# More products by seven in the MLP's down projection, sums of weights made sooner, activations by pairs of chunks

## Chip, cores, metric

The kernel runs on one core of one Trainium2 chip. The metric is device microseconds (us) of one execution, the median of several runs. Its engines go by their short names in the profile: PE is TensorE's matmul and PEld its weight load, DVE is VectorE, ACT is ScalarE, POOL is GpSimd, SP is SyncE, which issues nearly all DMAs.

## What is computed

One encoder block over 256 tokens of 2048 features, in float32, of which the reference's body is this:

```python
h = rms_norm(x, attn_norm[i])
proj = h @ w_in[i]
qa, ka, va, qb, kb, vb, ga, gb = jnp.split(proj, split_points, axis=-1)
ya = windowed_gqa(qa, ka, va, rel_bias_table, sink_a[i])
yb = dilated_attention(qb, kb, vb, rel_bias_table)
merged = jax.nn.sigmoid(ga) * (ya @ w_branch_a[i]) + jax.nn.sigmoid(gb) * (yb @ w_branch_b[i])
x = x + merged @ w_out[i]
hf = rms_norm(x, ffn_norm[i])
g = dwconv_centred(hf @ w_ffn_gate[i], conv_w[i], conv_b[i])
x = x + (jax.nn.gelu(g) * (hf @ w_ffn_up[i])) @ w_ffn_down[i]
gate_p = jax.nn.sigmoid(rms_norm(x, ple_norm[i]) @ w_ple_gate[i])
x = x + gate_p * (p[i] @ w_ple_proj[i])
return rms_norm(x, final_norm)
```

The change touches the last six lines: the gated MLP (2048 to 5632 and back, with a convolution of width 3 over the tokens on the gate's path and a tanh form of gelu), the embedding p (256 features) with its gate, and the last norm.

## The kernel before

**Number format.** Every operand of a matmul is split into a high part that TensorE multiplies in one pass and a low part, the remainder: ScalarE copies the high part out of a float32 tile (`nc.scalar.activation(hi, src, AF.Copy)`, line 264), VectorE subtracts it (line 265). A product takes three matmuls (`thirds`, lines 365 to 367: high by high, high by low, low by high), or two in the E stages (line 308 512 columns wide, line 315 256 wide).

**Stages.** The weights come as a list of pieces of 128 x 2048 values (1 MB), grouped by stages that TensorE does in order: A (input projections and attention), B0 to B3 with ba and bb (branch gates and projections), D0 and D1 (w_out), then twice, for each half of the 44 chunks of the MLP, E (gate and up products, `mlp` behind each) and F0, F1 (down projection to the left and the right half of the 2048 columns): E0, F00, F01, E1, F10, F11. At the end stand pp0 and pp1 (p by w_ple_proj) and G0, G2, G3 (the gate of p).

**Products by seven.** B, D, F and G0 are stages of quads: a piece is a 2 x 2 block of weights for two chunks of features and two strips of 512 columns. A piece marked s is multiplied directly: eight products, 24 matmuls of 512 columns. A piece marked S uses Strassen's scheme in Winograd's form: seven products, 21 matmuls. It pays with sums. Of the weights, VectorE makes four units out of a raw tile instead of two: unit n of 512 columns, unit n of 1024, then three differences in place (lines 257 to 259, one 1024 wide, two 512 wide), and units T13 and T24 of 1024 each. Of the activations, `sums_of` makes four sums of a pair of chunks. Of the results, `row_sums` adds the accumulators M1, M5, M6, M7 at the stage's end. An s piece needs the accumulators M2, M3, M4 and P22 alone, an S piece M1 to M7. `DOWN = "SsSsSsSsSss"` gives the eleven pairs of each F stage their kinds.

**Buffers that order the work.** PSUM has eight banks, each a tag with one buffer: M2 0, M3 1, M4 2, M1 3, M7 4, M5 5, M6 6, P22 7. A new tile in a bank waits until the last reader of the tile before it is done. Units of weights have rings: six of kind n (names uh, ul), two of kind T (vh, vl); raw tiles have three buffers. `pump` makes the next unit whenever a slot is dropped. Pieces of work that belong to another stage are hung up with `at((stage, piece, product), f)` and issued there by `run_due`; a scheduler then arranges each engine's instructions, whose queues run in order.

**Around the end.** xr holds the rows (2 x 128 tokens x 2048). When F10 has finished the left half of xr, `rows_pair` turns it back into columns: per group of two chunks four transposes on TensorE into one bank, then for each chunk ScalarE writes the high part of pl (line 472) and VectorE the low part (line 473). The four groups of the left half are hung up in F11 at (0,6), (1,2), (1,5) and (2,1) and all use the bank of P22; the four of the right half come at pp0, through M2, M3, M4 and P22. `combine` makes the sums of pl's pairs for G0, in a tile named pair with two buffers. `load_last` loads p (256 KB) into a tile of the name pair at piece 2 of F10, and `split_last` splits it at piece 9 into small tiles t and u. `quads("F11", ...)` has its own accumulator P22, opened by its first s piece, and reads it in line 936 (`residual`'s `finish`) behind the last matmul.

**The tail.** G3's last two products for the second 128 tokens are done in two halves of 256 columns, so that the left half is ready before the right. Behind them come, per 128 tokens, tanh, the addition into xr, squares, the sum `known`, the gains (line 1115), v (line 1112), the power on POOL (line 1114), the scaling by r and the output.

Of the kernel before, what the change touches and what calls it, by code (L numbers as in the profile page):

```python
# [16 lines left out]
P = 128  # L17
T = 256
# [70 lines left out]
JOINT = 4  # L89
JOINED = 2  # L90
# [4 lines left out]
DOWN = "SsSsSsSsSss"  # L95
# [3 lines left out]
def _ffn(half):  # L99

    jobs = []
    for f in range(FHALF + 1):
        if f < FHALF:
            jobs.append(("g", half * FHALF + f))
        if f:
            jobs.append(("u", half * FHALF + f - 1))
    return jobs


def _pieces():  # L110
# [29 lines left out]
    for half in range(2):  # L140
# [6 lines left out]
        for s in range(2):  # L147
            quads("F%d%d" % (half, s), ("w_ffn_down", 2 * s * WIDE), ("w_ffn_down", (2 * s + 1) * WIDE),
                  DOWN, half * FHALF)
# [38 lines left out]
def _encoder(ctx: ExitStack, tc, xt, pt, xrow, cols, gainrow, table, onehot, mask, ident_in, wts, out):  # L188
# [58 lines left out]
    def produce():  # L247
# [7 lines left out]
        if kind == "T13":  # L255
            q = [raw[:, i * WIDE:(i + 1) * WIDE] for i in range(4)]
            nc.vector.tensor_tensor(raw[:, :2 * WIDE], raw[:, WIDE:3 * WIDE], raw[:, :2 * WIDE], op=ALU.subtract)  # L257
            nc.vector.tensor_tensor(q[2], q[2], q[0], op=ALU.subtract)
            nc.vector.tensor_tensor(q[3], q[3], q[2], op=ALU.subtract)
# [6 lines left out]
        made[u] = (hi, lo)  # L266
        state["unit"] = u + 1
# [94 lines left out]
    def thirds(acc, stationary, w, first, last):  # L362

        (sh, sl), (wh, wl) = stationary, w
        nc.tensor.matmul(acc, sh, wh, start=first, stop=False, skip_group_check=True)  # L365
        nc.tensor.matmul(acc, sh, wl, start=False, stop=False, skip_group_check=True)  # L366
        nc.tensor.matmul(acc, sl, wh, start=False, stop=last, skip_group_check=True)  # L367
# [4 lines left out]
    def quad_stage(stage, moving, combos=None, tags=("M2", "M3", "M4", "P22")):  # L372
# [24 lines left out]
        for i, p in enumerate(pieces):  # L397
# [24 lines left out]
    def wide_stage(stage, moving, names, joint=1):  # L422
# [3 lines left out]
        ends = []  # L426
        alone = len(pieces) - joint
        for i, span in [(i, 1) for i in range(alone)] + [(alone, joint)]:
            g = 0
            for t in range(2):  # L430
                for c in range(4 * span):
# [5 lines left out]
                    if 1 < joint == span and t and c >= 4 * span - 2:  # L437
                        ends.append((part(moving(k), t), w))
                        continue
# [3 lines left out]
            for h in range(2) if ends else ():  # L443
                for e, (stationary, w) in enumerate(ends):
                    cs = slice(h * T, (h + 1) * T)
                    thirds(accs[1][:, cs], stationary, [a[:, cs] for a in w], False, e == 1)
            if ends:
                drop(_UNITS_OF[pieces[-1]][1])
# [4 lines left out]
    def gather(acc, scale=1.0, u=None, keep=lambda ins: ins):  # L453
# [3 lines left out]
        if u is None:  # L457
            u = sc.tile([P, T], F32, name="u")
# [32 lines left out]
    def diagonal(r):  # L491

        dg = sc.tile([P, T], F32, name="rdg", bufs=1)
# [75 lines left out]
    for step in order:  # L569
# [9 lines left out]
        while 4 * done + 5 < state["at"] // FIRST:  # L579
# [278 lines left out]
    def combine(key, m, pair, tag):  # L858

        u = held["tok"].tile([P, 2, T], F32, name="pair", bufs=2)  # L860
# [112 lines left out]

    def mlp(kind, n, acc):
        tok = held["tok"]
        if kind == "g":
            if n % 2 == 0:
                held["gw"] = tok.tile([P, 4, T], F32, name="gw", tag="c%d" % (n // 2 % 2 + 1))
            c, w = (held["gw"][:, 2 * (n % 2) + i] for i in range(2))
            u = gather(acc)  # L980
            nc.vector.tensor_tensor(u, u, rt[1], op=ALU.mult)
            nc.vector.tensor_scalar(c, u, tap(1, n), tap(3, n), op0=ALU.mult, op1=ALU.add)
            nc.vector.scalar_tensor_tensor(c[:, 1:], u[:, :-1], tap(0, n), c[:, 1:], op0=ALU.mult, op1=ALU.add)
            nc.vector.scalar_tensor_tensor(c[:, :-1], u[:, 1:], tap(2, n), c[:, :-1], op0=ALU.mult, op1=ALU.add)
            nc.scalar.activation(w, c, AF.Square)
            nc.vector.tensor_scalar(w, w, 0.044715, 1.0, op0=ALU.mult, op1=ALU.add)
# [191 lines left out]
```

## Time and profile before

| | |
|---|---|
| median of 3 runs | 1457.38 us (1457.35 to 1457.71) |
| profiled execution | 1457.96 us, of which 1456.2 us is the span from the first to the last instruction |
| granted TensorE clock, mean | 0.998 |
| busy PE, DVE, ACT | 1444.5, 1248.8, 822.1 us |
| E0, F00 with F01, E1 | about 628 to 875, 875 to 988, 988 to 1233 us |
| F10 with F11 | about 1233 to 1347 us |
| last matmul | at 1445.64 us |

In a row of the timeline stand the start in us, the duration in us, the engine, the line, the operation, the output and the inputs by name, the shape and how many instructions the row joins; in square brackets the idle time before it and what ended it. Engines with a q behind their name (SPq, ACTq) are issuing DMAs. Durations of neighbouring instructions on an engine overlap by some tens of ns, so what an instruction costs its engine is read from start to start. A row of windows gives for a stretch its length and each engine's busy time with the number of instructions in brackets.

### The profile page before, as it was taken

The numbers are of one execution on the slowest core, as the hardware profiler recorded it, in microseconds if no ns is written. First come the engines' busy times: TensorE is split into PE (matmuls) and PEld (weight loads), VectorE is DVE, ScalarE is ACT, GpSimd is POOL, SyncE is SP. The second block draws the span as 40 slices with busy tenths as digits, with TensorE's granted clock in tenths as the row PEclk, the third lists the DMA queues.
The fourth block names the chain that finished last, engine by engine and source line by source line (L and its number), as shares of the span: only waits on it lengthen the run. The fifth ranks groups of instructions, "written<-read, shape, count | busy, mean of one in ns | idle before, by whom it ended". The sixth has DMA issues, their size and how long they took to land.

```text
span 1456.2 us, 19520 instructions
## 1 busy us (share of the span) xinstructions
PE 1444.5 (99%) x7488; PEld 1235.9 (85%) x7488; DVE 1248.8 (86%) x1849; ACT 822.1 (56%) x1141; POOL 4.1 (0%) x9
## 2 busy tenths in 40 slices
PE   9999999999999999999999999999999999999997
PEld 8888888888888888888888888888888888888785
DVE  7677665679998989989888899989888889999995
ACT  7455544446555656666555555455555555565762
POOL 0000000000000000000000000000000000000000
PEclk9999999999999999999999999999999999999999
DMA  9654444535546456465554545565555554546462
GB/s 335 249 206 146 152 168 175 175 141 203 192 187 235 180 213 234 174 232 193 186 199 175 202 152 221 176 254 183 199 184 193 185 192 173 193 191 234 170 237 81
DMA packets 46312, 282.88 MB, mean 194 GB/s; under 512 B 4932, under 2 KB 9668, under 8 KB 13964
## 3 DMA queue, kind: packets, MB, share of 16 engines
q1 hardware_dynamic: 45500, 280.46, 53.2%
q8 instruction: 58, 0.95, 0.3%
q10 hardware_dynamic: 720, 1.19, 0.2%
q14 instruction: 34, 0.28, 0.1%
HBM read 279.49 MB, written 2.14 MB: 193 GB/s over the span
## 4 chain that ended last, share of the span: by engine, by line
PE 97%; DVE 1%; ACT 1%; issue 1%; DMA 0%; SPq 0%; POOL 0%; POOLq 0%; DVEq 0%; ACTq 0%
PE bank L308 29%; PE bank L315 15%; PE bank L365 14%; PE bank L366 14%; PE bank L367 14%; PE bank L354 2%; PE bank L356 2%; PE bank L355 2%; PE bank L292 1%; PE bank L293 1%; PE bank L870 1%; PE bank L687 0%; PE bank L635 0%; PE bank L634 0%; PE bank L633 0%
## 5 line engine op out<-in xcount | busy, mean ns | idle before, releaser
L264 ACT ACTIVATE uh<-raw 128x1024 fp32r<-128x1024 f32 (+2 forms) x518 | 522.3, 1017 | 399.5 <-PE bank L308 183.6
L265 DVE TENSOR_TENSOR ul<-raw,uh 128x1024 fp32r<-128x1024 f32 (+2 forms) x518 | 596.8, 1169 | 128.9 <-ACT uh L264 68.8
L308 PE MATMUL bank<-hf,uh 128*128 128x512 f32 x1408 | 336.3, 391 | 0.0
L308 PEld LDWEIGHTS bank<-hf,uh 128*128 128x128 f32 x1408 | 258.9, 188 | 50.2
L315 PEld LDWEIGHTS bank<-hf,ul 128*128 128x128 f32 x1408 | 180.4, 191 | 6.7
L315 PE MATMUL bank<-hf,ul 128*128 128x256 f32 x1408 | 182.8, 283 | 0.0
L264 ACT ACTIVATE vh<-raw 128x1024 fp32r<-128x1024 f32 x92 | 97.4, 1058 | 57.0 <-DVE raw L257 25.4
L265 DVE TENSOR_TENSOR vl<-raw,vh 128x1024 fp32r<-128x1024 f32 x92 | 111.9, 1219 | 0.4
L308 PE MATMUL bank<-hs,uh 128*128 128x512 f32 x432 | 103.6, 392 | 0.0
L456 ACT ACTIVATE t<-bank 128x256 f32<-128x256 f32 x122 | 46.5, 384 | 96.6 <-PE bank L315 89.5
L308 PEld LDWEIGHTS bank<-hs,uh 128*128 128x128 f32 x432 | 79.5, 188 | 15.6
L365 PE MATMUL bank<-uh,act 128*128 128x512 f32 x232 | 90.4, 390 | 0.0
L366 PE MATMUL bank<-ul,act 128*128 128x512 f32 x232 | 90.4, 390 | 0.0
L367 PE MATMUL bank<-uh,act 128*128 128x512 f32 x232 | 90.3, 389 | 0.0
L365 PE MATMUL bank<-uh,hs 128*128 128x512 f32 x172 | 67.3, 391 | 0.0
L367 PE MATMUL bank<-uh,hs 128*128 128x512 f32 x172 | 67.3, 391 | 0.0
L366 PE MATMUL bank<-ul,hs 128*128 128x512 f32 x172 | 67.1, 390 | 0.0
L257 DVE TENSOR_TENSOR raw<-raw 128x1024 f32<-128x1024 f32 x46 | 56.1, 1221 | 0.6
L315 PE MATMUL bank<-hs,ul 128*128 128x256 f32 x432 | 56.6, 284 | 0.0
L315 PEld LDWEIGHTS bank<-hs,ul 128*128 128x128 f32 x432 | 54.5, 191 | 1.0
L366 PE MATMUL bank<-vl,S 128*128 128x512 f32 x138 | 54.1, 392 | 0.1
L365 PE MATMUL bank<-vh,S 128*128 128x512 f32 x138 | 54.1, 398 | 0.0
(240 smaller groups left out, 2273.2 us busy)
## 6 DMA issues: line engine op xcount, KB each, us to landing
raw<-in_wts SPq DMA_DIRECT2D x251, 1024.0 KB, 4.8
raw<-in_wts SPq DMA_DIRECT2D x12, 512.0 KB, 7.2
xr<-in_xrow SPq DMA_DIRECT2D x4, 512.0 KB, 8.3
x<-in_xt SPq DMA_DIRECT2D x13, 128.0 KB, 6.0
hb<-hold SPq DMA_DIRECT2D x3, 514.0 KB, 5.9
hb<-hold SPq DMA_DIRECT2D x2, 768.0 KB, 7.5
last<-in_gainrow SPq DMA_DIRECT2D x1, 1024.0 KB, 6.9
out<-xr SPq DMA_DIRECT2D x4, 256.0 KB, 2.6
```

The source lines that it names most:

```text
L257: nc.vector.tensor_tensor(raw[:, :2 * WIDE], raw[:, WIDE:3 * WIDE], raw[:, :2 * WIDE], op=ALU.subtract)
L264: nc.scalar.activation(hi, src, AF.Copy)
L265: nc.vector.tensor_tensor(lo, src, hi.bitcast(F32), op=ALU.subtract)
L308: nc.tensor.matmul(acc, weights(u)[0][:, o * P:(o + 1) * P], m, start=first, stop=False, skip_group_check=True)
L315: nc.tensor.matmul(acc[:, T:], weights(u)[1][:, o * P:(o + 1) * P], m[:, :T], start=False, stop=last, skip_group_check=True)
L354: nc.tensor.matmul(acc[:, :n * P], xh, hi, start=(k == 0), stop=False)
L355: nc.tensor.matmul(acc[:, :n * P], xh, lo, start=False, stop=False)
L356: nc.tensor.matmul(acc[:, :n * P], xl, hi, start=False, stop=(k == KC - 1))
L365: nc.tensor.matmul(acc, sh, wh, start=first, stop=False, skip_group_check=True)
L366: nc.tensor.matmul(acc, sh, wl, start=False, stop=False, skip_group_check=True)
L367: nc.tensor.matmul(acc, sl, wh, start=False, stop=last, skip_group_check=True)
L456: keep(nc.scalar.activation(t, acc[:, T:], AF.Copy, scale=scale))
```

## The change

1. `DOWN` becomes a table by half and strip: F00, F01 and F10 get SSsSsSsSsSs (six S of eleven, the first two in a row), F11 gets sSsSsSsSsSs (five S, s first). The sums of activations are made for the pairs 0, 1, 3, 5, 7, 9. In all, nine matmuls of 512 fewer.
2. The differences of weights of an S piece are issued when its second unit n is made, no longer when the first unit T is.
3. M4 comes ahead of M2 and M3 in an S piece.
4. `mlp` works on pairs of chunks: products are gathered one by one, but the convolution, gelu and the split are done for two chunks at once; the first tap goes from VectorE to ScalarE. An up product comes two gate products later instead of one (LAG).
5. The tile pair has one buffer instead of two. p is loaded at piece 5 of F11 and split at piece 10, into one tile p in the place of S4.
6. G3's half columns go. In the tail, v is computed ahead of the gains, in program order.
7. Small: u of `gather` and the tile rdg have other buffers; squares in the first norm come later.

```diff
-DOWN = "SsSsSsSsSss"
+DOWN = (("SSsSsSsSsSs", "SSsSsSsSsSs"), ("SSsSsSsSsSs", "sSsSsSsSsSs"))
+PAIRS = (0, 1, 3, 5, 7, 9)
...
-        if kind == "T13":
-            q = [raw[:, i * WIDE:(i + 1) * WIDE] for i in range(4)]
-            nc.vector.tensor_tensor(raw[:, :2 * WIDE], raw[:, WIDE:3 * WIDE], raw[:, :2 * WIDE], op=ALU.subtract)
...
         made[u] = (hi, lo)
+        if _PIECES[p][0] == "S" and u == _UNITS_OF[p][1]:
+            q = [raw[:, i * WIDE:(i + 1) * WIDE] for i in range(4)]
+            nc.vector.tensor_tensor(raw[:, :2 * WIDE], raw[:, WIDE:3 * WIDE], raw[:, :2 * WIDE], op=ALU.subtract)
...
-                        ("M6", sums[1], 3, 0, None), ("M2", part(b, 0), 1, 1, None), ("M3", sums[3], 1, 0, 1),
-                        ("M4", part(b, 1), 3, 1, 3))):
+                        ("M6", sums[1], 3, 0, None), ("M4", part(b, 1), 3, 1, 3),
+                        ("M2", part(b, 0), 1, 1, None), ("M3", sums[3], 1, 0, 1))):
...
-        u = held["tok"].tile([P, 2, T], F32, name="pair", bufs=2)
+        u = held["tok"].tile([P, 2, T], F32, name="pair", bufs=1)
...
     def load_last():
-        held["pr"] = held["tok"].tile([P, 2, T], F32, name="pair", bufs=2)
+        held["pr"] = held["tok"].tile([P, 2, T], F32, name="pair", bufs=1)
         keep(nc.sync.dma_start(held["pr"], pt))
 
     def split_last():
-        for k in range(2):
-            ph_.append(sc.tile([P, T], FR, name="t"))
-            pl_.append(sc.tile([P, T], FR, name="u"))
-            nc.scalar.activation(ph_[k], held["pr"][:, k], AF.Copy)
-            nc.vector.tensor_tensor(pl_[k], held["pr"][:, k], ph_[k].bitcast(F32), op=ALU.subtract)
+        h = held["tok"].tile([P, 2, 2, T], FR, name="p", tag="S4")
+        held["p"] = h
+        nc.scalar.activation(h[:, 0], held["pr"], AF.Copy)
+        nc.vector.tensor_tensor(h[:, 1], held["pr"], h[:, 0].bitcast(F32), op=ALU.subtract)
...
-            at(("F10", 2, 0), load_last)
-            at(("F10", 9, 0), split_last)
+            at(("F11", 5, 0), load_last)
+            at(("F11", 10, 0), split_last)
...
-        nc.vector.tensor_scalar(v, ssq[:, t, 4:], known[:, t:t + 1], 1.0 / D, op0=ALU.add, op1=ALU.mult)
+        keep(nc.vector.tensor_scalar(v, ssq[:, t, 4:], known[:, t:t + 1], 1.0 / D, op0=ALU.add, op1=ALU.mult))
         r = sc.tile([P, 1], F32, name="r3")
         nc.gpsimd.tensor_tensor(r, v, mhalf[:, :1], op=ALU.pow)
-        nc.vector.tensor_tensor(xr[:, t, cut[3]], xr[:, t, cut[3]], gains[:, cut[3]], op=ALU.mult)
+        keep(nc.vector.tensor_tensor(xr[:, t, cut[3]], xr[:, t, cut[3]], gains[:, cut[3]], op=ALU.mult))
```

What it moves, engine by engine. First TensorE at the end of F11, before: bank_11899 is P22, bank_12299 and bank_12307 are pp0's, bank_11919 is the fourth group's.

```order
L367 MATMUL bank_11899<-uh_12169,act2_8950 128x512
L365 MATMUL bank_12299<-uh_12178,t_11713 128x512
L366 MATMUL bank_12299<-ul_12179,t_11713 128x512
L367 MATMUL bank_12299<-uh_12178,u_11714 128x512
L365 MATMUL bank_12299<-uh_12197,t_11717 128x512
L366 MATMUL bank_12299<-ul_12198,t_11717 128x512
L367 MATMUL bank_12299<-uh_12197,u_11718 128x512
L365 MATMUL bank_12307<-uh_12178,t_11713 128x512
L366 MATMUL bank_12307<-ul_12179,t_11713 128x512
L367 MATMUL bank_12307<-uh_12178,u_11714 128x512
L870 MATMUL bank_11919<-ident_75,xr_4916 128x128 x4
```

pp0 follows F11 at once; one group of the left half stands nine matmuls into it. The same place after the change: bank_11587 is P22, bank_11615, bank_11649 and bank_11671 are the second, third and fourth group of the left half, bank_12071, bank_12085 and bank_12097 are groups of the right half, bank_12233 and bank_12237 are G0's.

```order
L369 MATMUL bank_11587<-uh_11923,act2_8835 128x512
L862 MATMUL bank_12071<-ident_75,xr_4919 128x128
L862 MATMUL bank_12085<-ident_75,xr_4919 128x128
L862 MATMUL bank_12097<-ident_75,xr_4919 128x128
L862 MATMUL bank_11615<-ident_75,xr_4919 128x128 x4
L862 MATMUL bank_11649<-ident_75,xr_4919 128x128 x4
L862 MATMUL bank_12071<-ident_75,xr_4919 128x128 x3
L862 MATMUL bank_12085<-ident_75,xr_4919 128x128 x3
L862 MATMUL bank_12097<-ident_75,xr_4919 128x128 x3
L862 MATMUL bank_11671<-ident_75,xr_4919 128x128 x4
L367 MATMUL bank_12233<-uh_12037,pl_11556 128x512
L368 MATMUL bank_12233<-ul_12038,pl_11556 128x512
```

After fifteen matmuls of G0, with the last group (bank_12111) among them, pp0 begins with `L367 MATMUL bank_12056<-uh_11953,p_11992 128x512`. Three groups of the left half have moved behind F11, and pp0 behind them.

Second, VectorE behind F11 after the change, from the reading of P22 (line 928) on. pair_11775 is the tile of pl's pair 2, c_11996 a sum of accumulators.

```order
L928 TENSOR_TENSOR xr_4919<-xr_4919,bank_11587 128x512
L267 TENSOR_TENSOR raw_11951<-raw_11951 128x512
L262 TENSOR_TENSOR vl_12045<-raw_11951,vh_12044 128x1024
L465 SCALAR_TENSOR_TENSOR pl_11556<-bank_11615,cl_73,pl_11556 128x256
L268 TENSOR_TENSOR raw_11951<-raw_11951 128x512
L465 SCALAR_TENSOR_TENSOR pl_11556<-bank_11615,cl_73,pl_11556 128x256
L930 TENSOR_TENSOR xr_4919<-xr_4919,c_11996 128x1024
L262 TENSOR_TENSOR vl_12049<-raw_11951,vh_12048 128x1024
L465 SCALAR_TENSOR_TENSOR pl_11556<-bank_11649,cl_73,pl_11556 128x256
```

Before the change the rows of pl for the second and third group stood in F11; here they are spread over VectorE's other work behind it.

Third, SyncE around p's load after the change:

```order
L246 DMA raw_11964<-in_wts 128x2048
L246 DMA raw_12031<-in_wts 128x2048
L246 DMA raw_12123<-in_wts 128x2048
L1015 DMA pair_11810<-in_pt 128x512
L246 DMA raw_12183<-in_wts 128x2048
L1055 DMA last_12055<-in_gainrow 128x2048
```

and before it:

```order
L244 DMA raw_11396<-in_wts 128x2048
L244 DMA raw_11431<-in_wts 128x2048
L1006 DMA pair_11441<-in_pt 128x512
L244 DMA raw_11475<-in_wts 128x2048
L244 DMA raw_11509<-in_wts 128x2048
```

The load has moved down the queue from F10 to just ahead of the gains' load, with one raw tile between them; its tile pair_11810 takes the buffer of pair_11775.

More of the change, by code (lines that the diff above doesn't have):

```diff
@@ L101, in _ffn @@
     jobs = []
-    for f in range(FHALF + 1):
+    for f in range(FHALF + LAG):
         if f < FHALF:
             jobs.append(("g", half * FHALF + f))
-        if f:
-            jobs.append(("u", half * FHALF + f - 1))
+        if f >= LAG:
+            jobs.append(("u", half * FHALF + f - LAG))
     return jobs
```

97 lines of the change are left out of this document (52 added, 45 removed).

## The prediction

> **What bounds the kernel now.** I read the page first: the busy line and the chain that ended last.
>
> ```profile
> PE 1444.5 (99%) x7488; PEld 1235.9 (85%) x7488; DVE 1248.8 (86%) x1849; ACT 822.1 (56%) x1141; POOL 4.1 (0%) x9
> PE 97%; DVE 1%; ACT 1%; issue 1%; DMA 0%; SPq 0%; POOL 0%; POOLq 0%; DVEq 0%; ACTq 0%
> ```
>
> TensorE carries 97% of the chain. The view of the waits, asked for TensorE alone, leaves nothing else:
>
> ```profile
> PE bank L225 <- DVE mhalf L220: 1.1, 1, 1.1
> PE bank L293 <- DVE ul L265: 0.3, 1, 0.3
> ```
>
> So between its start and the last matmul TensorE waits 1.4 us in all, and the end moves only by matmuls taken away, by waits newly made, and by the tail behind the last matmul. The windows by stage say how close VectorE follows (columns: length, then busy time and count of PE, PEld, DVE, ACT, POOL; granted clock, DMA share, GB/s). The four stretches are E0, F00 with F01, E1, F10 with F11:
>
> ```profile
> 628.00:875.00 247.00, 247.00 (x1427) 218.33 (x1427) 219.42 (x394) 142.03 (x216) 0.71 (x1) 1.00 0.53 189
> 875.00:988.00 113.00, 113.00 (x500) 93.43 (x500) 103.12 (x115) 60.76 (x67) 0.00 (x0) 1.00 0.57 210
> 988.00:1233.00 245.00, 245.00 (x1410) 216.56 (x1409) 216.70 (x379) 136.11 (x203) 0.00 (x0) 1.00 0.53 187
> 1233.00:1346.00 113.00, 113.00 (x505) 93.34 (x504) 107.92 (x132) 66.52 (x80) 0.00 (x0) 1.00 0.56 206
> ```
>
> TensorE is full in all four; VectorE has 28 us to spare in each E stage, 10 in F00 with F01, 5 in F10 with F11. A matmul of 512 columns takes 113.00 / 500 = 0.226 us.
>
> **The change part by part.**
>
> *MLP activations by pairs, LAG.* They take VectorE work out of E0 and E1, where 247.00 and 245.00 us of TensorE stand over 219.42 and 216.70 of VectorE. No matmul goes, so the worth is nothing. The cover is those 28 us; were it gone, the cost would show as TensorE waits in E, and the work only shrinks there.
>
> *Three more products by seven.* F00, F01 and F10 each turn one s piece (24 matmuls) into an S (21): 9 x 0.226 = -2.0 us on TensorE. VectorE pays for it. Its pace is read from start to start in the rows behind F11, which the largest term needs as well:
>
> ```profile
> 1347.38 0.68 DVE L936 TENSOR_TENSOR xr<-xr,bank 128x512 f32<-128x512 f32 x1
> 1347.97 0.68 DVE L265 TENSOR_TENSOR ul<-raw,uh 128x512 fp32r<-128x512 f32 x1
> 1348.58 0.68 DVE L936 TENSOR_TENSOR xr<-xr,bank 128x512 f32<-128x512 f32 x1
> 1349.18 1.22 DVE L257 TENSOR_TENSOR raw<-raw 128x1024 f32<-128x1024 f32 x1
> 1350.31 1.21 DVE L265 TENSOR_TENSOR ul<-raw,uh 128x1024 fp32r<-128x1024 f32 x1
> 1351.44 0.47 DVE L473 SCALAR_TENSOR_TENSOR pl<-bank,cl,pl 128x256 fp32r<-128x256 f32 x1
> 1351.84 0.68 DVE L258 TENSOR_TENSOR raw<-raw 128x512 f32<-128x512 f32 x1
> ```
>
> A 1024-wide operation costs 1.13 us of VectorE, a 512-wide one 0.61, a row of pl 0.40. An S piece has four of the first kind and three of the second, 6.35; an s piece has two of the first, 2.26; each exchange adds 4.1. In F00 with F01 VectorE then has 103.12 + 8.2 = 111.3 us against 113.00 - 1.4 = 111.6 of TensorE: no slack. The stages now begin with two S in a row, behind the other stage's finishing adds. At F00's start the rings are full, since VectorE was early in E0; at F01's they are not. I take +1.0 us for the boundaries, from 0 (the rings hold enough) to 3. The sums made sooner, and M4 ahead of M2 and M3, change which of these operations comes first and not their number; they lie in that bound.
>
> *The end of F11: the large term.* The pattern of F11 now begins with s, whose products go into M2, M3, M4 and P22, so bank 7 belongs to the accumulator P22 from the first piece on, until VectorE has read it behind the last matmul. `rows_pair` turns its groups through the same bank. Of four groups before, three ran inside F11 and only the last behind it. Now only the first is inside: the order of TensorE shows the second and third right behind F11's last matmul, then the fourth, then the eighth, and all of pp0 behind those. They are serial through one bank: four transposes, ScalarE's two pl, VectorE's two, each in its queue's order. Before, only one group stood so, and pp0 covered its wait:
>
> ```profile
> 1346.99 0.39 PE L367 MATMUL bank<-uh,act 128*128 128x512 f32 x1
> 1347.22 0.39 PE L365 MATMUL bank<-uh,t 128*128 128x512 f32 x1
> ...
> 1349.08 0.39 PE L367 MATMUL bank<-uh,u 128*128 128x512 f32 x1
> 1349.31 0.66 PE L870 MATMUL bank<-ident,xr 128*128 128x128 f32 x4
> 1349.72 0.48 PE L365 MATMUL bank<-uh,t 128*128 128x512 f32 x1
> ...
> 1356.08 1.48 PE L870 MATMUL bank<-ident,xr 128*128 128x128 f32 x12
> ```
>
> and the p tile that pp0 needs had been loaded and split in F10:
>
> ```profile
> 1242.58 1.46 SPq L244 DMA_DIRECT2D raw<-in_wts  x2
> 1244.09 0.42 SPq L1006 DMA_DIRECT2D pair<-in_pt  x1
> 1252.59 0.75 DVE L1013 TENSOR_TENSOR u<-pair,t 128x256 fp32r<-128x256 f32 x2
> ```
>
> pp0 begins at 1347.22; P22 is read from 1348.58, and the four transposes follow at 1349.31 with nine matmuls of pp0 ahead of them. Why can't pp0 cover now? Its p tile has become a buffer of `pair`, which has one buffer instead of two; its load is queued on SyncE behind the last reading of pair 2 of pl, and that pair needs the third group. So pp0 waits for the very chain that it should hide.
>
> Four more rows price ScalarE's share and the small sums:
>
> ```profile
> 1346.74 0.64 ACT L264 ACTIVATE uh<-raw 128x512 fp32r<-128x512 f32 x1 [3.19 <-PE bank L367]
> 1357.11 1.54 ACT L472 ACTIVATE pl<-bank,cl 128x256 fp32r<-128x256 f32 x4
> 1364.73 0.28 DVE L847 TENSOR_TENSOR cmb<-pair 128x128 f32<-128x128 f32 x1
> 1364.93 0.28 DVE L848 TENSOR_TENSOR cmb<-pair 128x128 f32<-128x128 f32 x1
> ```
>
> The chain, from the end of F11 as 0, by VectorE's order and the paces above (four transposes 0.41, from 1349.31 to 1349.72):
> - VectorE ends the 1024-wide add (L930) at 0.6, then one ul of 512, one of 1024 and a raw difference of 1024 before it reads P22: 0.6 + 0.61 + 1.13 + 1.13 + 0.61 = 4.1.
> - Second group: transposes 4.1 to 4.5, ScalarE's two pl (0.4 each, begun as the bank lands) by 5.7; VectorE has 0.61 + 1.13 + 0.40 + 0.61 + 0.40 to its second pl: 7.25.
> - Third group: from 7.3; VectorE has two of 1024 and four pl: 7.25 + 2.26 + 1.60 = 11.1, with a wait for ScalarE, which squares a 1024-wide row meanwhile, 11.35.
> - Fourth group: from 11.4. Beside it pair 2's add and its four small sums (0.61 and 0.2 each) and pl rows; the last reading of the pair at 14.45.
> - SyncE issues p at 14.5. What it takes is bounded by these rows of DMA issues (the last column is the time to landing):
>
> ```profile
> out<-xr SPq DMA_DIRECT2D x4, 256.0 KB, 2.6
> pair<-in_pt SPq DMA_DIRECT2D x1, 256.0 KB, 7.5
> raw<-in_wts SPq DMA_DIRECT2D x251, 1024.0 KB, 4.8
> ```
>
> The 7.5 was this same load, issued at 1244.09 right behind the two raw loads of 1242.58. Now the raw load ahead of it starts some 5 us earlier, at the T24 subtraction (9.6), and needs 4.8, so I take the 2.6 of the undisturbed 256 KB: 17.1. [...]
> - ScalarE's 512-wide split 0.6: pp0's first matmul at 17.75.
>
> Meanwhile TensorE has nine plus six matmuls of G0 (15 x 0.226 = 3.4) and 28 transposes (28 x 1.48 / 12 = 3.4), all of which it had to do in before as well. Wait: 17.75 - 6.8 = 10.9 us. Behind it, pp0 and pp1 are 48 matmuls without a need of VectorE, which is 10.9 us ahead then; I see no further wait. If ScalarE and VectorE keep their pace the bound below is 9 (the two short waits fall out); with the 7.5 us load it is 15.8.
>
> *The tail.* The last third of the product loses its half columns: twelve matmuls of 256 become six of 512.
>
> ```profile
> 1445.38 0.90 ACTq L1122 DMA_DIRECT2D out<-xr  x2
> 1445.64 0.28 PE L367 MATMUL bank<-uh,pl 128*128 128x256 f32 x1
> 1446.32 0.84 ACT L1106 ACTIVATE c<-bank,rh 128x256 f32<-128x256 f32 x2 [0.97 <-PE bank L367]
> ...
> 1448.90 0.15 DVE L1111 TENSOR_TENSOR known<-known,ssq 128x1 f32<-128x1 f32 x1
> 1449.01 0.69 DVE L1115 TENSOR_TENSOR xr<-xr,last 128x512 f32<-128x512 f32 x1
> 1449.62 0.21 DVE L1112 TENSOR_SCALAR v<-ssq,known 128x1 f32<-128x1 f32 x1
> 1449.91 0.55 POOL L1114 TENSOR_TENSOR r<-v,mhalf 128x1 f32<-128x1 f32 x1 [5.32 <-DVE v L1112]
> ```
>
> The halves were to let tanh begin early, but ScalarE was issuing the first rows' output until 1445.38 + 0.90 = 1446.28. Now v comes right behind known: 1449.62 - 1449.01 = 0.6 us sooner, twice; the first rows' issues go 0.6 sooner too, so tanh can follow the last matmul, about 0.4 sooner. The gains then lie beside POOL's 0.55. Together -1.0 us (0 to -1.2).
>
> **Sum.** -2.0 + 1.0 + 10.9 - 1.0 = +8.9 us on the profiled execution's 1457.96, which stands 0.6 above the median 1457.38; the forecast is the median's: 1466.3.
>
> **The rivals.**
>
> *The p load stays slow* (7.5 instead of 2.6): +4.9, 1471.2. For it, the row above; against it, that the raw load ahead has landed by then. Chance 0.15.
>
> *The clock drops.* TensorE waits 3.7 us (0.4 to 4.1) and then works in short bursts. Behind the last matmul, which ends at 1445.92, the granted clock (third from last) goes:
>
> ```profile
> 1448.00:1449.00 1.00, 0.00 (x0) 0.00 (x0) 1.00 (x6) 0.00 (x0) 0.00 (x0) 1.00 0.77 285
> 1449.00:1450.00 1.00, 0.00 (x0) 0.00 (x0) 0.83 (x3) 0.00 (x0) 0.09 (x1) 0.50 0.00 0
> ```
>
> It halves some 3 us into idleness. At half the clock the four groups of transposes on the chain cost 4 x 0.41 = 1.6 more, and if it stayed halved behind the chain for 3 to 6 us, half of that is lost: +1.6 to +4.6, about 1469.5. The Trainium skill (TensorE: Matmul & The Clock Gate, section What's actually happening) says that one idle window of about 3.4 us halves the clock and one busy window restores it, with windows that run freely; by that rule the first gap just reaches the limit. The rows agree with half the clock; no row shows a gap of this size amid work. Chance 0.2.
>
> *The chain is covered (the other side).* If the bank came free earlier, or p were there when F11 ends, pp0's 48 matmuls (10.9 us) would fill the wait as they do at 1347.22, and -2.0 - 1.0 with 0 to 1 for the boundaries stay: 1454.4 to 1455.4, say 1455.1. It decides where P22's read to pp0's first matmul takes less than the 6.8 us of TensorE work in between. The profile speaks against it: pp0 ran there because t and u were split at 1252.59, and the order now has p's load behind the chain. Chance 0.07.
>
> *VectorE becomes the bound in F00 and F01* (111.3 against 111.6, with worse packing): up to 3 us more on top, 1469. Chance 0.1.
>
> **How the numbers follow.** The forecast holds 0.48, from 1462.5 (short chain, 9, without boundary stalls) to 1468. The range reaches over the clock, the slow load and VectorE: 1462.5 to 1472. Left out are the covered chain and two of the slow mishaps together. A measurement of this kernel tells about 0.2%, 2.9 us, from no change. The covered chain gives -2 to -3, at the edge: 0.05 same and 0.03 faster; all else is slower, 0.92.
>
> **What would show it.** Right: waits of TensorE for pl, xr or p between F11's last matmul and pp0's first, of about 11 us in four steps; transposes of the second group right behind F11; the p load issued some 14 us after F11's end and landed within 3. Nine fewer matmuls of 512 and no waits inside E0 and E1. v at once behind known. Wrong: pp0 within 7 us of F11's end, or TensorE waits for ul or vl inside F00 and F01 of more than 3 us.

## The result, and the profile after

The changed kernel takes 1468.28 us (median of 6 runs, 1466.85 to 1469.76) against 1457.37 us of the kernel before (6 runs, 1456.79 to 1457.71): a ratio of 1.0073, 95% interval 1.0062 to 1.0084. It is 0.7% slower; the forecast was 1466.3, from 1462.5 to 1472.0. The profiled execution took 1468.22 us, its span is 1466.4 us.

The page's chain of the changed kernel by engine, and then the waits of TensorE (what waited, for whom, us in all, how often, longest):

```profile
PE 91%; DVE 7%; issue 1%; ACT 0%; DMA 0%; POOLq 0%; POOL 0%; DVEq 0%; ACTq 0%
```

```profile
PE bank L862 <- DVE pl L465: 3.4, 2, 2.2
PE bank L862 <- DVE xr L928: 3.0, 1, 3.0
PE bank L227 <- DVE mhalf L222: 1.1, 1, 1.1
PE bank L862 <- DVE xr L930: 0.6, 1, 0.6
PE bank L367 <- ACT uh L261: 0.3, 1, 0.3
PE bank L367 <- DVE c L818: 0.3, 1, 0.3
PE bank L368 <- DVE ul L262: 0.3, 1, 0.3
```

VectorE has risen from 1% of the chain to 7%. Line 862 is the transposes of `turn_back`: they wait 3.0 us for the reading of P22 (line 928) and twice for the rows of pl (line 465). All of it lies at one place, as TensorE's timeline behind F11 shows (start, duration, what; in brackets the idle time ahead and who ended it):

```profile
1344.28 0.39 PE L369 MATMUL bank<-uh,act 128*128 128x512 f32 x1
1345.29 0.55 PE L862 MATMUL bank<-ident,xr 128*128 128x128 f32 x3 [0.62 <-DVE xr L930]
1348.81 1.11 PE L862 MATMUL bank<-ident,xr 128*128 128x128 f32 x4 [2.97 <-DVE xr L928]
1352.13 3.23 PE L862 MATMUL bank<-ident,xr 128*128 128x128 f32 x13 [2.20 <-DVE pl L465]
1356.57 1.09 PE L862 MATMUL bank<-ident,xr 128*128 128x128 f32 x4 [1.22 <-DVE pl L465]
1357.31 0.78 PE L367 MATMUL bank<-uh,pl 128*128 128x512 f32 x1
1357.88 0.63 PE L368 MATMUL bank<-ul,pl 128*128 128x512 f32 x1
1358.31 0.63 PE L369 MATMUL bank<-uh,pl 128*128 128x512 f32 x1
...
1359.59 0.63 PE L369 MATMUL bank<-uh,S 128*128 128x512 f32 x1
1360.02 1.06 PE L862 MATMUL bank<-ident,xr 128*128 128x128 f32 x4
1361.41 0.92 PE L367 MATMUL bank<-uh,pl 128*128 128x512 f32 x2 [0.34 <-ACT uh L261]
1362.67 0.50 PE L368 MATMUL bank<-ul,pl 128*128 128x512 f32 x1 [0.34 <-DVE ul L262]
...
1364.24 0.40 PE L369 MATMUL bank<-vh,pl 128*128 128x512 f32 x1
1364.48 0.40 PE L367 MATMUL bank<-uh,p 128*128 128x512 f32 x1
```

F11's last matmul starts at 1344.28 and is done 0.23 later; pp0's first starts at 1364.48, where the kernel before went on at once (1346.99 and 1347.22). The three groups stand one behind the other, at 1348.81, 1352.13 and 1356.57, each released by VectorE. And a row of four transposes lasts 1.11 us where it lasted 0.66 before (at 1349.31); the matmul of 1357.88 is followed by the next 0.43 later, not 0.23. The windows give the reason (third column from the end: the granted clock):

```profile
1347.00:1348.00 1.00, 0.00 (x0) 0.00 (x0) 1.00 (x2) 0.00 (x0) 0.00 (x0) 1.00 0.00 0
1348.00:1349.00 1.00, 0.19 (x1) 0.19 (x2) 1.00 (x3) 0.81 (x1) 0.00 (x0) 0.59 0.00 0
1360.00:1361.00 1.00, 1.00 (x5) 0.67 (x4) 0.31 (x1) 0.70 (x1) 0.00 (x0) 0.50 0.02 6
1361.00:1362.00 1.00, 0.66 (x3) 0.49 (x2) 0.61 (x1) 1.00 (x3) 0.00 (x0) 0.58 0.62 211
1362.00:1363.00 1.00, 0.66 (x3) 0.30 (x2) 1.00 (x2) 1.00 (x3) 0.00 (x0) 1.00 0.12 45
```

The clock falls to half at about 1348.2, some 3.7 us behind F11, and comes back at about 1361.8. For p there are two rows, SyncE's issue and what the view of the tile pair says of its landing:

```profile
1359.94 0.33 SPq L1015 DMA_DIRECT2D pair<-in_pt  x1
DMA to landing us min/median/max: 2.6/2.6/2.6
```

The issue comes 15.4 us behind F11's end. But it isn't p that pp0 waits for in the end. pp0's first matmul follows without a wait on the fifteen matmuls of G0 that stand ahead of it in TensorE's order, and the last seven of these could start only at 1362.67, behind VectorE's ul, which needs ScalarE's uh, which the matmul of 1359.59 released:

```profile
1360.30 1.06 ACT L261 ACTIVATE uh<-raw 128x1024 fp32r<-128x1024 f32 x1 [1.10 <-PE bank L369]
1361.39 1.23 DVE L262 TENSOR_TENSOR ul<-raw,uh 128x1024 fp32r<-128x1024 f32 x1 [1.08 <-ACT uh L261]
1362.61 0.63 ACT L1020 ACTIVATE p<-pair 128x512 fp32r<-128x512 f32 x1
```

p's high half, the last row, is done at 1363.24, 1.2 us before pp0 starts. That pp0 stands behind these matmuls at all comes with the late p: where p has its own place, as in the second experiment, it stands ahead of them.

The rest of the kernel is seen best by the lengths of its stretches, taken in the timelines from first matmul to first matmul (in F10 and F11 to the start of F11's last; all in us):

| kernel | start to E0 | E0 | F00, F01 | E1 | F10, F11 | F11's last to pp0's first | F11's last to the kernel's last matmul |
|---|---|---|---|---|---|---|---|
| before | 627.83 | 247.10 | 112.96 | 244.91 | 114.19 | 0.23 | 98.65 |
| after | 626.47 | 247.08 | 112.82 | 244.91 | 113.00 | 20.20 | 111.80 |
| F11 begins with S | 627.43 | 247.08 | 112.83 | 244.90 | 114.36 | 0.22 | 98.78 |
| p in its own place | 627.28 | 247.09 | 112.84 | 244.90 | 113.11 | 0.23 | 99.46 |

Up to E0 all changed kernels do the same and still differ by 1.2 us from profile to profile (626.29 to 627.51 in the profiles of this study), so most of the 1.4 us by which after is ahead there can be scatter. All twelve are ahead of the one profile of before, by 0.3 to 1.5 us; whether the change gains some tenths there is open. The span grew by 10.2 us: 13.15 behind F11's last matmul, less 1.36 up to E0, 0.14 in F00 and F01, 1.19 in F10 and F11 and 0.24 in the tail.

### The profile page after: what moved, and what is told of

Its sections match the earlier page's. It is cut to its first block, busy times and chain, and to the rows that moved or that the text cites. A ratio compares the mean times of both kernels' runs of the same rounds, so it can differ in the third digit from the quotient of the medians.

```text
span 1466.4 us, 19308 instructions
## 1 busy us (share of the span) xinstructions
PE 1447.3 (99%) x7473; PEld 1237.1 (84%) x7473; DVE 1214.4 (83%) x1657; ACT 841.6 (57%) x1130; POOL 4.9 (0%) x9
## 3 DMA queue, kind: packets, MB, share of 16 engines
q10 hardware_dynamic: 720, 1.19, 0.2%
## 4 chain that ended last, share of the span: by engine, by line
PE 91%; DVE 7%; issue 1%; ACT 0%; DMA 0%; POOLq 0%; POOL 0%; DVEq 0%; ACTq 0%
PE bank L310 28%; PE bank L317 14%; PE bank L367 13%; PE bank L368 12%; PE bank L369 12%; DVE ul L262 3%; PE bank L356 2%; PE bank L358 2%; PE bank L294 2%; PE bank L357 2%; DVE vl L262 1%; PE bank L295 1%; DVE raw L266 1%; PE bank L862 1%; PE bank L679 0%
## 5 line engine op out<-in xcount | busy, mean ns | idle before, releaser
L261 ACT ACTIVATE vh<-raw 128x1024 fp32r<-128x1024 f32 x98 | 103.5, 1057 | 72.8 <-DVE raw L266 59.0
L262 DVE TENSOR_TENSOR vl<-raw,vh 128x1024 fp32r<-128x1024 f32 x98 | 119.4, 1220 | 0.2
L368 PE MATMUL bank<-ul,act 128*128 128x512 f32 x214 | 83.1, 390 | 0.0
L369 PE MATMUL bank<-uh,act 128*128 128x512 f32 x214 | 83.0, 389 | 0.0
L367 PE MATMUL bank<-uh,act 128*128 128x512 f32 x214 | 82.5, 390 | 0.0
L367 PE MATMUL bank<-uh,hs 128*128 128x512 f32 x172 | 67.5, 392 | 0.0
L266 DVE TENSOR_TENSOR raw<-raw 128x1024 f32<-128x1024 f32 x49 | 59.8, 1220 | 0.4
L367 PE MATMUL bank<-vh,S 128*128 128x512 f32 x147 | 57.4, 398 | 0.3 <-DVE c L818 0.3
L368 PE MATMUL bank<-vl,S 128*128 128x512 f32 x147 | 57.4, 390 | 0.0
L369 PE MATMUL bank<-vh,S 128*128 128x512 f32 x147 | 57.1, 390 | 0.0
```

The lines of the kernel that those rows point to most:

```text
L262: nc.vector.tensor_tensor(lo, src, hi.bitcast(F32), op=ALU.subtract)
L367: nc.tensor.matmul(acc, sh, wh, start=first, stop=False)
L368: nc.tensor.matmul(acc, sh, wl, start=False, stop=False)
L369: nc.tensor.matmul(acc, sl, wh, start=False, stop=last)
```

## The experiments

My theory was that the wait needs two things at once: the bank of P22, which the s at F11's start takes away from the groups, and p's load, which the one buffer of pair puts behind the same chain. The rivals were one of the two alone, or VectorE as the bound.

**F11 begins with S.** The first cure alone; p stays in the tile pair.

```diff
-DOWN = (("SSsSsSsSsSs", "SSsSsSsSsSs"), ("SSsSsSsSsSs", "sSsSsSsSsSs"))
+DOWN = (("SSsSsSsSsSs", "SSsSsSsSsSs"), ("SSsSsSsSsSs", "SssSsSsSsSs"))
```

> The changed kernel with one edit: F11's pattern begins with S again (SssSsSsSsSs, five S as before), so that P22 is opened in its second piece; p stays in the tile pair with its late load. My theory (the wait of 13 us needs both: the bank of P22 taken from F11's first piece on, and p's load behind pair 2 of pl): three groups of transposes run inside F11, pp0 follows F11's last matmul within 1 us, 1455.5 to 1458 us. Rival A (p's buffer alone makes the wait): p is still loaded late into pair, so the wait stays, above 1464. Rival B (VectorE is simply the bound in F10 and F11, 111.4 of 113 us busy, and whatever is put back into F11 stalls it there): 1460 to 1464, with TensorE waiting for ul or vl inside F11.

Measured: 1456.91 us (before 1457.72 on the same chip; ratio 0.9995, 0.9986 to 1.0004). pp0 follows F11 at once. SyncE's row of p's load, and TensorE's at the end of F11:

```profile
1321.66 0.43 SPq L1015 DMA_DIRECT2D pair<-in_pt  x1
```

```profile
1346.60 0.39 PE L369 MATMUL bank<-uh,act 128*128 128x512 f32 x1
1346.82 0.39 PE L367 MATMUL bank<-uh,p 128*128 128x512 f32 x1
```

One S moved by one place in a pattern, with as many S and as many matmuls, takes the whole wait away, though p still goes through pair. But p isn't late any more, as the expectation had it: its load is issued 25 us ahead of F11's last matmul, because pair 2 of pl is now read inside F11. So the one buffer of pair makes p late only when the groups are late. Rival A is out, and so is B: TensorE waits for no ul or vl in F11.

**p in its own place.** The second cure alone, with the split of p one piece sooner; F11 still begins with s.

```diff
-        held["pr"] = held["tok"].tile([P, 2, T], F32, name="pair", bufs=1)
+        held["pr"] = held["tok"].tile([P, 2, T], F32, name="pr", tag="c1")
...
-            at(("F11", 10, 0), split_last)
+            at(("F11", 9, 0), split_last)
```

> The changed kernel with one edit: p is loaded into the buffer of c1, which is free in the middle of F11, and not into pair; it is split one piece sooner. F11 still begins with s, so three groups of the left half still stand behind F11 and are serial through one bank. My theory: pp0 and pp1 (48 matmuls, 10.9 us) now follow F11 at once and cover most of the chain; 1456 to 1460 us. Rival C (the serial chain through P22's bank holds G0 whatever fills the time, p's place is a side issue): 1463 to 1468. The granted clock stays at 1.00 behind F11 if the gaps are gone.

Measured: 1456.76 us (0.9993, 0.9985 to 1.0002). The three groups still stand behind F11, but pp0 and pp1 run between them:

```profile
1345.45 0.39 PE L367 MATMUL bank<-uh,p 128*128 128x512 f32 x1
...
1350.14 0.60 PE L862 MATMUL bank<-ident,xr 128*128 128x128 f32 x4
1350.50 0.48 PE L368 MATMUL bank<-ul,p 128*128 128x512 f32 x1
...
1354.01 1.58 PE L862 MATMUL bank<-ident,xr 128*128 128x128 f32 x13
1355.34 0.48 PE L368 MATMUL bank<-ul,p 128*128 128x512 f32 x1
```

The chain through one bank is even a little longer than in the changed kernel (the third group starts 8.6 us behind F11's end, there 7.6), and costs nothing where other work is ready. So the bank taken early is harmless while p has its own place, the shared buffer is harmless while the groups run early, and either cure alone is enough: the theory holds, and rival C falls too. The two causes aren't independent, though: in the changed kernel the first is what makes the second bite. The rest of the change, without its wait, is worth 0.8 to 1.0 us, which is within what a measurement can tell from nothing.

**Six S in F11 as well, and the tail.** The first kernel gives F11 the pattern of the others, the second adds an edit in the tail.

```diff
-DOWN = (("SSsSsSsSsSs", "SSsSsSsSsSs"), ("SSsSsSsSsSs", "sSsSsSsSsSs"))
+DOWN = (("SSsSsSsSsSs", "SSsSsSsSsSs"), ("SSsSsSsSsSs", "SSsSsSsSsSs"))
```

> The changed kernel with F11 as the other three stages: SSsSsSsSsSs, six S, three matmuls fewer than the change (-0.7 us); P22 is opened in the third piece, behind all four groups. My theory: no wait behind F11; but F10 and F11 get one S more, and VectorE, which had 1.6 us to spare there with the groups moved out, has to take 4 us for the S and some 5 us for the groups and the sums of pl back; 1456 to 1460 us, with TensorE waiting for VectorE at the start of F11. If VectorE's time were no matter there, 1455. Rival A (p's buffer alone): above 1464.

```diff
-        keep(nc.vector.tensor_tensor(xr[:, t, cut[3]], xr[:, t, cut[3]], gains[:, cut[3]], op=ALU.mult))
...
+            elif n == 3:
+                nc.vector.scalar_tensor_tensor(row, row, r, gains[:, cut[3]], op0=ALU.mult, op1=ALU.mult)
```

> The kernel before this one, with one more edit in the tail: the gains of the last 512 columns are multiplied in the same VectorE instruction as r, so that VectorE does nothing while GpSimd computes r. In the changed kernel GpSimd's power took 0.93 us beside VectorE's gains, 0.55 us before, when it ran alone. If the two disturb each other, the power takes 0.55 again and the time falls by 0.3 to 0.6 us against the kernel before; if the power's 0.93 has another cause, it stays at 0.93 and the time moves by less than 0.2 us.

Measured: 1461.29 us (1.0023, 1.0014 to 1.0032) and 1459.55 us (1.0015, 1.0006 to 1.0024). The first lies above the 1456 to 1460 that were expected. Three matmuls fewer cost time: F10 and F11 take 116.74 and 116.52 us where they took 114.36 with five S in F11. The stall is VectorE's, as expected, and it spills into G0. The waits of the first of the two kernels:

```profile
PE bank L367 <- DVE pl L465: 1.4, 1, 1.4
PE bank L368 <- DVE vl L262: 1.2, 2, 1.0
```

The edit in the tail does what it should. GpSimd's power, in the changed kernel beside VectorE's gains and in this one alone:

```profile
1459.69 0.68 DVE L1122 TENSOR_TENSOR xr<-xr,last 128x512 f32<-128x512 f32 x1
1459.85 0.93 POOL L1121 TENSOR_TENSOR r<-v,mhalf 128x1 f32<-128x1 f32 x1 [4.79 <-DVE v L1119]
1460.82 0.72 ACT L1126 ACTIVATE xr<-xr,r 128x512 f32<-128x512 f32 x1 [3.19 <-POOL r L1121]
```

```profile
1451.25 0.21 DVE L1119 TENSOR_SCALAR v<-ssq,known 128x1 f32<-128x1 f32 x1
1451.54 0.55 POOL L1121 TENSOR_TENSOR r<-v,mhalf 128x1 f32<-128x1 f32 x1 [5.05 <-DVE v L1119]
```

But the two medians differ by 1.7 us, more than the 0.3 to 0.6 expected. The waits of both are alike; the clock is not. In the 30 us behind F11, first the kernel without and then the one with the edit in the tail:

```profile
1346.00:1376.00 30.00, 28.45 (x125) 22.50 (x124) 28.89 (x45) 22.24 (x35) 1.07 (x1) 0.94 0.60 214
```

```profile
1346.00:1376.00 30.00, 28.42 (x131) 22.37 (x130) 28.88 (x45) 23.52 (x37) 1.07 (x1) 1.00 0.57 207
```

In the first, the clock halves behind a wait of 1.36 us in G0 and eight matmuls are slow, in the second a wait of 1.38 us at the same place leaves it alone. Runs of the first kernel lie between 1459.6 and 1462.2, of the second between 1458.9 and 1461.7. What of the 1.7 us is the tail's can't be read from these times; the rows say 0.4 (0.93 to 0.55).

**The first gap filled.** 30 idle transposes behind F11, to keep the clock up; they leave no work out and their result isn't used.

```diff
+    spare = bank("M5")
+    for _ in range(30):
+        nc.tensor.transpose(spare[:, :P], ident, ident)
```

> The changed kernel with 30 idle transposes of the unit matrix (some 3.7 us) into the free bank M5 right behind F11's last matmul; their result is not used. They take away no wait: the chain through P22's bank and p's load stay as they are. They only keep TensorE busy in the first gap. If the halved clock cost time (my second rival): it stays at 1.00 through the first gap, pp0 begins 17.5 to 18.5 us behind F11's last matmul and not 20.2, and the time is 1465.5 to 1467 us. If the clock is a side show and VectorE and ScalarE alone set the pace: pp0 at 20 us or later, 1468 to 1469.

Measured: 1468.48 us (1.0074, 1.0061 to 1.0087), as the changed kernel. Of the two outcomes that were expected, the time is that of the second, the clock as a side show; but the edit tests only a part of it. Two windows of this kernel:

```profile
1352.00:1354.00 2.00, 0.63 (x4) 0.42 (x4) 2.00 (x4) 1.53 (x2) 0.00 (x0) 1.00 0.00 0
1354.00:1356.00 2.00, 1.61 (x8) 1.61 (x9) 2.00 (x5) 1.90 (x5) 0.00 (x0) 0.56 0.00 0
```

The clock holds through the first gap and halves only at about 1354.2, 9 us behind F11's last matmul (1345.40), after the second gap of 2.6 us; pp0 starts 20.0 us behind that matmul, not 18. In the first 9 us the chain moves at the pace of VectorE and ScalarE, and a TensorE at full clock gains nothing: the third group starts 7.7 us behind F11's end and the fourth 11.9, in the changed kernel 7.6 and 12.1. The fourth group and the six matmuls of G0 behind it, which lie on the path to pp0, run at half clock here as well; what that costs was not tested by itself.

**What the additional S pieces are worth.** All four F stages with the old pattern of five S, and six S with the two in a row at the end; both without the wait behind F11.

```diff
-PAIRS = (0, 1, 3, 5, 7, 9)
-DOWN = (("SSsSsSsSsSs", "SSsSsSsSsSs"), ("SSsSsSsSsSs", "sSsSsSsSsSs"))
+PAIRS = (0, 2, 4, 6, 8)
+DOWN = (("SsSsSsSsSss", "SsSsSsSsSss"), ("SsSsSsSsSss", "SsSsSsSsSss"))
```

> The changed kernel with the old pattern SsSsSsSsSss in all four F stages: five S each, nine matmuls more than the change, P22 opened in the second piece, so without the wait behind F11; p still late through pair. Against the kernel that begins F11 with S (1456.9) it asks what the three additional S pieces are worth. If VectorE ate them (F00 with F01 took 112.82 us against 112.96 before, where six matmuls fewer are 1.36): within 0.6 of 1456.9. If they are worth their matmuls: 1458.5 to 1459.

```diff
+PAIRS = (0, 2, 4, 6, 8, 9)
+DOWN = (("SsSsSsSsSSs", "SsSsSsSsSSs"), ("SsSsSsSsSSs", "SsSsSsSsSss"))
```

> The changed kernel with six S in F00, F01 and F10 as SsSsSsSsSSs, the two in a row at the end and not at the start, and F11 as SsSsSsSsSss; as many matmuls as the change, no wait behind F11. If the stalls in F00 with F01 (1.0 us, most of it where F01 begins and its first S waits for a bank of F00's sums) come from SS at the start: F00 with F01 takes 111.8 us and the time is 1455.5 to 1456.3. If VectorE's total is the bound (111.3 of 111.6): the stalls only move, 1456.5 to 1457.5.

Measured: 1457.07 us (0.9996, 0.9987 to 1.0005) with five S, 1458.33 us (1.0004, 0.9995 to 1.0013) with SS at the end. So the nine matmuls saved, 2.0 us of TensorE, are worth 0.2 us, less than the scatter. In the changed kernel VectorE is busy for 111.72 of 112.82 us in F00 with F01, before for 103.12 of 113.00, so the reading is that VectorE ate them. The kernel with SS at the end is slower than either expectation had it: SS at the end shortens F00 with F01 to 112.24 us, 0.6 less than with SS at the start where 1.0 was expected, and loses 1.4 in F10 and F11 (115.74 against 114.36). The stalls move.

**Both cures and the tail.** F11 begins with S, p in the buffer of c1, gains with r.

> The changed kernel with F11's pattern beginning with S (SssSsSsSsSs), with p loaded into the buffer of c1, and with the gains of the last 512 columns in the same instruction as r. My theory: either of the first two takes the whole wait away, so the two together bring nothing over one (1456.9 and 1456.8 us alone); the tail brings 0.5: 1456.0 to 1456.6. Rival: the two waits add up and each cure alone left a part; then 1455 or less.

Measured: 1456.55 us (0.9993, 0.9984 to 1.0002), as the theory has it: the cures don't add up.

**GpSimd for VectorE.** Two tries to relieve VectorE, on top of the last kernel: the third difference of weights, and the additions of c into xr.

```diff
-            nc.vector.tensor_tensor(q[3], q[3], q[2], op=ALU.subtract)
+            (nc.gpsimd if p >= _STAGES["F00"][0] else nc.vector).tensor_tensor(q[3], q[3], q[2], op=ALU.subtract)
```

> The kernel with both cures and the tail (1456.55 us) with one edit: of the three differences of weights of an S piece, the last (512 wide) goes from VectorE to GpSimd in all stages from F00 on, 27 of them. The theory that VectorE's total eats the three additional S pieces (F00 with F01 112.84 us, where TensorE has 111.6 of work, VectorE 112.33 of 113 busy): VectorE has 7.3 us less to do in F00 with F01, that pair of stages falls to 111.7, and the time to 1454 to 1455.5. Rival: GpSimd and VectorE disturb each other, as the power beside the gains showed (0.93 against 0.55), VectorE's instructions beside the difference grow by as much as they save: 1456 to 1458, F00 with F01 at 112.8 or more.

```diff
-                nc.vector.tensor_tensor(xr[:, t, wide], xr[:, t, wide], held["c"][t], op=ALU.add)
+                (nc.gpsimd if stage in ("F00", "F01", "F10") else nc.vector).tensor_tensor(
+                    xr[:, t, wide], xr[:, t, wide], held["c"][t], op=ALU.add)
```

> The kernel with both cures and the tail (1456.55 us) with one edit: the addition of the sums c into xr, 1024 wide and two at the end of a stage, goes from VectorE to GpSimd for F00, F01 and F10, six in all. It takes 2.3 us of VectorE away just where F01 and F11 begin, where the first S piece waits. If the stalls lie at that place and not in VectorE's total: F00 with F01 at 112.0 us, the time 1455 to 1456. If the total counts: 4.5 of 112.3 us go too, about the same, 1455 to 1456, and the two can't be told apart by the time but by where TensorE waits. Rival, that GpSimd disturbs VectorE: 1456.5 or later, with VectorE's rows beside GpSimd's longer.

Measured: 1485.86 us (1.0190, 1.0176 to 1.0204) and 1464.56 us (1.0039, 1.0025 to 1.0053). Both rivals won, the first by far more than the 1456 to 1458 that it claimed. A difference on GpSimd in the first kernel, and VectorE's instruction beside it:

```profile
890.18 1.30 POOL L268 TENSOR_TENSOR raw<-raw 128x512 f32<-128x512 f32 x1 [10.13 <-DVE raw L267]
890.43 2.13 DVE L262 TENSOR_TENSOR vl<-raw,vh 128x1024 fp32r<-128x1024 f32 x1 [0.48 <-ACT vh L261]
892.48 1.21 DVE L262 TENSOR_TENSOR ul<-raw,uh 128x1024 fp32r<-128x1024 f32 x1
```

GpSimd takes 1.30 us for what costs VectorE 0.61, and VectorE's subtraction beside it takes 2.13 instead of 1.21: it loses more than it was spared, and vh, which needs the difference, comes later (TensorE waits 5.1 us for vh in this kernel). In the second kernel GpSimd takes 2.4 to 3.4 us for an addition 1024 wide, which costs VectorE 1.13; TensorE waits 1.5 us for GpSimd's result and 2.6 us for vl.

**The best of it.** The changed kernel with p in the buffer of c1, the gains with r, the first 128 tokens' output issued by SyncE alone, and two of the last four rows scaled by ScalarE.

```diff
-            if n == 1:
+            if n == 1 or n == 0 and t:
                 nc.scalar.activation(row, row, AF.Copy, scale=r)
...
-            (nc.scalar if n % 2 else nc.sync).dma_start(out[:, t, cut[n]], row)
+            (nc.scalar if n % 2 and t else nc.sync).dma_start(out[:, t, cut[n]], row)
```

> The best parts together: the changed kernel with p in the buffer of c1 (1456.76 us alone, where F10 to the last matmul took 0.6 us less than with F11 beginning with S), the gains in the same instruction as r, and two more edits in the tail: the first 128 tokens' output is issued by SyncE alone, so that ScalarE's tanh for the second 128 needn't wait for its own DMA issues (0.3 us), and ScalarE scales two of the last four rows and not one (0.3 us of VectorE). My sum: 1456.76 - 0.4 - 0.3 - 0.3 = 1455.8; 1455.3 to 1456.3, that is 0.1% under the kernel before. Rival: the order of the output's landings sets the end and not the last row's arithmetic; then 1456.3 to 1456.8.

Measured: 1456.04 us (before 1457.67; 0.9990, 0.9981 to 0.9999): 0.1% faster than the kernel before, at the edge of what the interval tells from nothing, and 0.8% faster than the change. The sum of the expectation, 1455.8, was near, but the three small edits weren't measured apart: from the last matmul to the end they bring 0.5 us in the profiles (9.83 against 10.30 with p in its own place alone), not 1.0.

## Why the prediction was right, and where its sizes were off

**The end of F11** was the step that decided, and it went as written up to p's landing, down to the order of the three waits. From the end of F11 (1344.51):

| step | forecast | measured |
|---|---|---|
| P22 is read, until | 4.1 | 4.2 |
| second group starts | 4.1 | 4.3 |
| third group starts | 7.3 | 7.6 |
| fourth group starts | 11.4 | 12.1 |
| p's load is issued | 14.5 | 15.4 |
| p has landed | 17.1 | 18.0 |
| p's high half is made, until | 17.75 | 18.7 |
| pp0's first matmul | 17.75 | 20.0 |

The paces of VectorE from rows of before carried the first four steps to within 0.7 us, and the load took the 2.6 us that the undisturbed row had, so the rival of the slow load is out. The experiments show the cause from both sides: either cure gives pp0 back at 0.2 us behind F11. Only the last step had the wrong path: the forecast let pp0 start when p was split, and TensorE's table of waits has none for p. G0's matmuls, which the forecast had only as 3.4 us of work to fill the time, were themselves held up by the chain, by ScalarE's uh and by VectorE's ul, and ended 1.2 us behind p's split.

**The clock** was named as a rival with a chance of 0.2, and it came: half the clock from 3.7 us behind F11 on. The forecast had set it as dear, +1.6 to +4.6, because transposes on the chain would take longer. They did (a row of four lasts 1.11 us, before 0.66), and up to the fourth group next to nothing of it counted: with the gap filled that group starts 0.2 us sooner. From there on it may have counted: from the fourth group to the start behind the six slow matmuls of G0 3.45 us pass (1356.57 to 1360.02), where the paces of before give 0.41 + 6 x 0.226 = 1.8. Without these 1.7 us G0 would have been done ahead of p's split, so my estimate is that some 1.2 us of the last 2.2 in the table go back to the clock, and the rest to steps of VectorE and ScalarE that came some tenths later each. No run tests it: the kernel with the filled gap runs this stretch at half clock too. The rule that I had cited from the Trainium skill (TensorE: Matmul & The Clock Gate, What's actually happening) is that an idle window of about 3.4 us halves the clock. The rows come near it at F11 and don't decide it: the clock falls 3.7 us behind the last matmul, but three transposes stand in that stretch, and TensorE is idle only for its last 2.3 us. The wait of 1.4 us that halved it in one kernel and not in another is shorter than that.

**The sum.** Wait and slow clock behind F11: 20.0 less the 6.8 us of work in between are 13.1 us, where the forecast had 10.9. About 1 us of it comes back later, and 12.2 are left. Before, six matmuls of pp0 and pp1 behind a transpose were longer (0.32 instead of 0.23, as from 1349.72 to 1350.04), and small waits stood in pp1 and G0; behind pp0's start the changed kernel has neither.

**The boundaries** were mis-sized: the forecast had +1.0 for VectorE's lack of slack, from 0 to 3. F00 with F01 lost 1.36 us of matmuls and became 0.14 shorter: +1.2. F10 and F11 lost 0.68 and gave away two groups, 8 transposes of 0.99, and became 1.19 shorter: +0.5. Together +1.7, most of the -2.0 that the three S pieces save; in the kernel whose F11 begins with S and keeps its three groups it is +2.1, all of it. The reason stood in the prediction (111.3 us of VectorE against 111.6 of TensorE), and should have led to the plain reading that a swap of 0.68 us of TensorE for 4.1 of VectorE brings next to nothing where VectorE has no slack.

**The tail** was mis-sized too: -1.0 forecast, -0.24 measured, from the last matmul's start to the end. v does come right behind known. But the gains, which I put beside GpSimd's 0.55, made it 0.93; from known to r it is 1.41 us (1459.37 to 1460.78) against 1.56 before. And as r came only that little sooner, ScalarE was still issuing the first rows' output when tanh could have begun (from 1455.85 for 0.90 us, and tanh starts at 1456.79).

**Luck.** The three terms each came out higher than forecast (12.2 for 10.9, +1.7 for +1.0, -0.24 for -1.0), some 2.7 us together: -2.0 + 1.7 + 12.2 - 0.2 is 11.6 (unrounded), not 8.9. The span grew by only 10.2 because the profiled execution of the changed kernel was 1.36 us ahead up to E0, of which the forecast knew nothing. So the number is nearer than its terms.

**The MLP by pairs** brings nothing, as forecast: E0 and E1 take 247.08 and 244.91 us, before 247.10 and 244.91, though VectorE is busy for 194.87 and 189.94 us in these windows instead of 219.42 and 216.70.

**The covered chain**, the rival on the other side, was priced at -2 to -3. The two kernels in which the chain is covered show it: 0.8 to 1.0 us faster. Its mechanism was right, and its price too high by the boundaries and the tail.

## What to carry to other kernels

A buffer that two stages share is a dependence: ask of each new first user (here a pattern's first letter) until when it holds the buffer, and who stands in the queue behind those that wait. A wait costs only what no ready work covers, so look what the covering work itself depends on; two things harmless by themselves, a bank taken earlier and a load that waits for a shared buffer, made some 12 us together, because the first made the second late. And work saved on the full engine is worth only the slack of the engine that pays for it.

## What was not expected of the hardware

GpSimd and VectorE hold each other up even in small instructions: a power of one element per partition took 0.93 us beside a 512-wide multiplication and 0.55 alone, and VectorE's subtraction took 2.13 us beside a difference on GpSimd and 1.21 alone. The Trainium skill (SBUF — State Buffer, Who interferes with whom) has this as a rule: VectorE's instructions with two inputs from SBUF contend with GpSimd's reads for a shared port, and the one that comes second waits. The runs agree: each of these VectorE instructions reads two tiles from SBUF, and the excess of 0.9 us is near what was left of GpSimd's 1.30 when VectorE began (1.05).

The clock halves behind less than full idleness: with six S in F11 it was at half from about 1366.8 to 1370.1, with no longer wait ahead of it than one of 1.36 us in G0 and one of 0.18 two matmuls earlier; with the edit in the tail on top, waits of 1.38 and 0.16 at the same places left it alone.
